# Two recurrences on one core: neighbouring chunks' state products issued in turn into two PSUM banks, and one pool of eight banks

## Chip, core and metric

The kernel runs on one core of a Trainium2 chip. The metric is the device time of one execution in microseconds (us), taken as the median of several runs. The engines are called as in the profile: PE (matrix products), PEld (the weight loads that go with them), DVE, ACT, POOL, and SP, whose queue issues most DMAs. PSUM, where products land, has eight banks here, each of 512 float32 values in 128 partitions.

## What is computed

Two blocks of two layers each act on 512 tokens of width 1024, all in float32. Almost all of the work is dense projections, cross-attention, sliding-window attention and feed-forward layers. One layer of each block holds a gated recurrence, computed by chunks. The first (HGRN2) has 4 heads, chunks of 32 tokens, key and value width 128:

```python
k_end = k * jnp.exp(b_last - b)
d_state = jnp.einsum('bhnsd,bhnsv->bhndv', k_end, v)   # state products, one per chunk and head
def step(state, inp):                                   # scan over the chunks
    dec, ds = inp
    return dec[..., None] * state + ds, state
...
o_inter = jnp.einsum('bhntd,bhndv->bhntv', q_t, s_start)
o = o_intra + o_inter
```

The second (GLA) has the same form with 4 heads, chunks of 64 tokens, key width 128 and value width 256.

## The kernel before

Tokens lie in four tiles of 128 (`t` = 0 to 3). Large projections are done at a split precision: each operand is a high and a low part in a 32-bit format that PE reads in one pass, and a product is three matmuls (`mm3`, lines 180 to 182). Weights arrive by DMA on SP, ACT makes the high part (line 152, or 172 with a gain) and DVE the low part (line 153 or 173). `lin_a` and `lin_b` hold four banks for one projection, with the contraction as the outer loop, and hand each bank to an evacuation on ACT or DVE at the end. `lin_out` with `between` (the output projections of the attentions and of the first mixer) holds four banks half accumulated while other work runs between its halves.

PSUM is divided by two pools. `bank` (line 125) takes projections, attention outputs and the readout's accumulator `po` from the pool `mm` of five banks; `xbank` (line 132) takes transposes, scores, cumulative sums and state products from the pool `aux` of three.

The program's text does not fix the order on the engines. A scheduler walks the instructions by priority (the text's order, moved by `high_priority`, `ahead` and `later`) against its own model of time, gives a tile a free bank of its pool when the first instruction on it is placed, and writes out one fixed order for each engine. On the chip each engine goes through its order and waits on semaphores.

The recurrence (`recur`, line 547) runs over the four tiles: `advance(t)` and then, one tile behind, `readout(t-1)`. `advance` transposes q and k (line 254, copied by ACT in lines 564 and 567), makes the scores of the four heads (line 570), masks them (line 573), and then goes over the chunks of the tile, four in HGRN2 and two in GLA. For each chunk the state products (line 581) of all its heads go into one bank (HGRN2) or two (GLA, two heads in each). A chunk's operands lie in its own rows: rows 0 to 31, 32 to 63 and so on in HGRN2, 0 to 63 and 64 to 127 in GLA, so that PE uses 32 or 64 rows of its array. Then DVE makes the new state of each head (line 588; line 586 for the first): old state times decay plus the product out of PSUM. `readout` adds the scores' part (line 605) and the states' part (line 608, one chunk's rows of the output at a time) in the bank `po`, and ACT squares and scales it (lines 612 and 616). The products are plain float32, and each stands in the trace as two records: 64 products in HGRN2 and 32 in GLA leave 192.

Beside the HGRN2 recurrence run the projections of its q and its gate, keys and values of the cross-attention, and a convolution of 31 taps, which DVE does in 90 instructions of low priority (line 525).

Of the kernel before, what the change touches and what calls it, by code (L numbers as in the profile page):

```python
# [10 lines left out]
F32 = mybir.dt.float32  # L11
# [3 lines left out]
ALU = mybir.AluOpType  # L15
# [57 lines left out]
class Net:  # L73
    def __init__(self, tc, a, ctx):
        self.tc, self.nc, self.a = tc, tc.nc, a
        pool = lambda name, bufs, **kw: ctx.enter_context(tc.tile_pool(name=name, bufs=bufs, **kw))
        self.const = pool("const", 1)
        self.wp = pool("wp", 4)
        self.rawp = pool("rawp", 3)
        self.big = pool("big", 16)  # L80
        self.work = pool("work", 2)
        self.small = pool("small", 4)
        self.mm = pool("mm", 5, space=bass.MemoryType.PSUM)
        self.aux = pool("aux", 3, space=bass.MemoryType.PSUM)
        self.n = 0
        nc = self.nc
        self.consts = self.const.tile([128, NCONST], F32, name="consts")
        nc.sync.dma_start(self.consts[:, :DEC], a["consts"][:, :DEC])
        self.ident = self.consts[:, IDENT:IDENT + 128]
        self.steps = self.const.tile([128, 256], F32R, name="steps")  # L90
        nc.scalar.activation(self.steps, self.consts[:, TRI:TRI + 256], AF.Copy)
        self.gains_T = self.const.tile([128, 40], F32, name="gains_T")
        self.half = self.const.tile([128, 8], F32, name="half")
        nc.gpsimd.memset(self.half, -0.5)
        self.r = []
        for t in range(4):
            self.r.append(self.const.tile([128, 1024], F32, name=f"r{t}"))
            nc.sync.dma_start(self.r[t], a["x"][0, t * 128:(t + 1) * 128, :])
            if t == 1:
                self.first = self.chunk(a["ab_w_in"][0], 2560, ahead=0)  # L100
# [29 lines left out]
        return bank  # L130

    def xbank(self, shape):
        return self.aux.tile(shape, F32, tag="aux", name=self.nm("aux"))

    def bload(self, dst, ap):
        self.nc.sync.dma_start(dst, ap.unsqueeze(0).broadcast_to(list(dst.shape)))
# [156 lines left out]
        else:  # L293
            self.nc.vector.tensor_tensor(r, r, ps, ALU.add)  # L294

# [1 line left out]

    def hgrn_mixer(self):
        nc, a = self.nc, self.a
# [259 lines left out]
    def advance(self, t, qt, kt, ke, vh, dec, before, tri, size, dv):  # L559
        nc = self.nc  # L560
        nch = 128 // size
        ps = self.transpose4(qt[:, t, :])
        qT = self.tmp().rearrange("p (h t) -> p h t", h=4)
        nc.scalar.activation(qT, ps, AF.Copy)
        ps = self.transpose4(kt[:, t, :])
        kT = self.tmp().rearrange("p (h t) -> p h t", h=4)
        nc.scalar.activation(kT, ps, AF.Copy)
        sc = self.xbank([128, 4, 128])
        for h in range(4):
            nc.tensor.matmul(sc[:, h, :], kT[:, h, :], qT[:, h, :], start=True, stop=True)  # L570
        P = self.masked[t % 2]
        mask = self.consts[:, tri:tri + 128].bitcast(I32).unsqueeze(1).broadcast_to([128, 4, 128])
        nc.vector.copy_predicated(P, mask, sc)
        new = self.slot([128, nch, 4, dv], name="S")
        per = 512 // dv
        for c in range(nch):
            rows = slice(c * size, c * size + size)
            for h0 in range(0, 4, per):
                d = self.xbank([128, per, dv])
                for h in range(h0, h0 + per):  # L580
                    nc.tensor.matmul(d[:, h - h0, :], ke[rows, t, h * 128:h * 128 + 128], vh(t, h)[rows, :],  # L581
                                     start=True, stop=True)
                for h in range(h0, h0 + per):
                    p = new[:, c - 1, h, :] if c else None if before is None else before[0][:, nch - 1, h, :]
                    if p is None:
                        nc.vector.tensor_copy(new[:, c, h, :], d[:, h - h0, :])
                    else:
                        nc.vector.scalar_tensor_tensor(new[:, c, h, :], p, dec[:, t, h, c:c + 1], d[:, h - h0, :],
                                                       ALU.mult, ALU.add)
        return new, qT, P  # L590

    def readout(self, t, got, before, vh, size, dv, out, po):
# [211 lines left out]
            first = False  # L804


# [1 line left out]

    def gla_prepare(self):
        nc, a = self.nc, self.a  # L810
# [312 lines left out]
```

## Time and profile before

| | before |
|---|---|
| runs | 2504.08, 2504.81, 2505.48 us (median 2504.81) |
| span of the profiled execution | 2503.4 us |
| PE busy | 2458.3 us (98%) |
| DVE busy | 1249.7 us (50%) |
| ACT busy | 944.6 us (38%) |
| POOL busy | 181.3 us (7%) |
| state products (line 581), PE busy | 30.4 us in 192 records |

The profiled execution has no time of its own beside its span. The span goes from its first to its last instruction, and the three runs lie 0.7 to 2.1 us above it. A busy PE is not PE at its peak, since matmuls overlap in the records: what an instruction costs is read from how far the next one starts behind it. PEclk is the share of its full clock that PE was granted.

### The profile page before, as it was taken

How to read it: one execution, taken by the hardware profiler on the slowest of the kernel's cores; microseconds unless marked ns; L12 is line 12 of the kernel's file. 1: busy time of each engine (PE TensorE's matmuls, PEld its weight loads, DVE VectorE, ACT ScalarE, POOL GpSimd, SP SyncE). 2: the span in 40 equal slices, each digit the busy share in tenths (PEclk: the TensorE clock that was granted, in tenths of full speed). 3: DMA queues.
4: the chain of work that ended last, by engine and by line, in shares of the span. 5: the costliest groups of instructions: out<-in, count | busy, mean ns of one | idle time of the engine just before them, and what ended most of it. 6: DMA issues, size and time to landing. Idle time of an engine off the chain costs nothing.

```text
span 2503.4 us, 30298 instructions
## 1 busy us (share of the span) xinstructions
PE 2458.3 (98%) x12334; PEld 2052.4 (82%) x12334; DVE 1249.7 (50%) x1772; ACT 944.6 (38%) x1576; POOL 181.3 (7%) x219
## 2 busy tenths in 40 slices
PE   8989999999999999999999999999999999999998
PEld 8876787888888997888888786888888877888887
DVE  4798566433326766433327423444444467444443
ACT  3643343222223343322224634433223456423323
POOL 1151300000000100000001003100000100000000
PEclk9999899999999999999999999999999999999999
DMA  6323122333324332233223223233222421222222
GB/s 214 109 102 102 53 85 77 92 99 95 99 74 144 123 130 76 85 101 99 95 76 121 69 85 43 76 101 101 93 101 98 142 74 51 72 97 95 99 93 84
DMA packets 121788, 239.48 MB, mean 96 GB/s; under 512 B 7849, under 2 KB 14309, under 8 KB 121392
## 3 DMA queue, kind: packets, MB, share of 16 engines
q1 hardware_dynamic: 118976, 229.73, 28.3%
q0 software_dynamic: 2096, 6.76, 1.4%
q8 instruction: 97, 1.59, 0.3%
q10 hardware_dynamic: 576, 1.05, 0.1%
q14 instruction: 43, 0.35, 0.0%
HBM read 234.34 MB, written 6.32 MB: 96 GB/s over the span
## 4 chain that ended last, share of the span: by engine, by line
PE 90%; DVE 6%; issue 1%; ACT 1%; DMA 1%; POOL 0%; SPq 0%; POOLq 0%; DVEq 0%; ACTq 0%
PE mm L180 28%; PE mm L181 27%; PE mm L182 27%; DVE acc L525 2%; PE aux L254 2%; PE aux L581 1%; DVE w L153 1%; PE aux L180 1%; PE mm L608 1%; PE mm L605 1%; PE aux L182 1%; PE aux L181 1%; DVE bn L275 0%; PE aux L1043 0%; DMA raw<-in_ffn_wg 0%
## 5 line engine op out<-in xcount | busy, mean ns | idle before, releaser
L153 DVE TENSOR_TENSOR w<-raw,w 128x1024 fp32r<-128x1024 f32 (+1 forms) x286 | 341.0, 1195 | 604.4 <-ACT w L152 604.1
L181 PE MATMUL mm<-xTl,w 128*128 128x512 f32 (+1 forms) x1696 | 614.0, 363 | 2.2 <-DVE xTl L153 2.2
L180 PE MATMUL mm<-xTh,w 128*128 128x512 f32 (+1 forms) x1696 | 610.4, 363 | 1.0 <-ACT w L152 0.8
L182 PE MATMUL mm<-xTh,w 128*128 128x512 f32 (+1 forms) x1696 | 605.7, 362 | 0.0
L152 ACT ACTIVATE w<-raw 128x1024 fp32r<-128x1024 f32 (+1 forms) x286 | 293.8, 1029 | 748.8 <-PE mm L182 598.3
L181 PEld LDWEIGHTS mm<-xTl,w 128*128 128x128 f32 x1696 | 321.5, 190 | 50.8 <-DVE xTl L153 2.4
L180 PEld LDWEIGHTS mm<-xTh,w 128*128 128x128 f32 x1696 | 320.9, 190 | 50.4 <-ACT w L152 1.2
L182 PEld LDWEIGHTS mm<-xTh,w 128*128 128x128 f32 x1696 | 319.4, 189 | 48.8
L181 PE MATMUL mm<-w,hidh 128*128 128x512 f32 x752 | 292.0, 389 | 0.0
L180 PE MATMUL mm<-w,hidh 128*128 128x512 f32 x752 | 291.1, 389 | 0.0
L182 PE MATMUL mm<-w,hidl 128*128 128x512 f32 x752 | 288.9, 389 | 0.0
L173 DVE SCALAR_TENSOR_TENSOR w<-raw,gains_T,w 128x512 fp32r<-128x512 f32 (+1 forms) x200 | 139.0, 738 | 212.0 <-ACT w L172 211.3
L172 ACT ACTIVATE w<-raw,gains_T 128x512 fp32r<-128x512 f32 (+1 forms) x200 | 131.3, 707 | 237.3 <-PE mm L182 220.9
L182 PEld LDWEIGHTS mm<-w,hidl 128*128 128x128 f32 x752 | 141.2, 188 | 29.3
L180 PEld LDWEIGHTS mm<-w,hidh 128*128 128x128 f32 x752 | 141.2, 188 | 29.2
L181 PEld LDWEIGHTS mm<-w,hidh 128*128 128x128 f32 x752 | 141.2, 188 | 29.1
L180 PE MATMUL mm<-w,xTh 128*128 128x512 f32 (+1 forms) x352 | 135.1, 386 | 0.0
L181 PE MATMUL mm<-w,xTh 128*128 128x512 f32 (+1 forms) x352 | 135.1, 384 | 0.0
L182 PE MATMUL mm<-w,xTl 128*128 128x512 f32 (+1 forms) x352 | 134.8, 384 | 0.0
L294 DVE TENSOR_TENSOR r<-r,mm 128x512 f32<-128x512 f32 x112 | 76.3, 686 | 72.8 <-PE mm L182 72.7
L525 DVE SCALAR_TENSOR_TENSOR acc<-u,pack,acc 128x511 f32<-128x511 f32 (+29 forms) x90 | 83.7, 972 | 0.0
L180 PEld LDWEIGHTS mm<-w,xTh 128*128 128x128 f32 x352 | 66.5, 189 | 15.5 <-issue 2.3
(323 smaller groups left out, 3344.9 us busy)
## 6 DMA issues: line engine op xcount, KB each, us to landing
raw<-in_w_up SPq DMA_DIRECT2D x64, 512.0 KB, 3.6
raw<-in_w_down SPq DMA_DIRECT2D x64, 512.0 KB, 3.2
raw<-in_ffn_wd SPq DMA_DIRECT2D x44, 512.0 KB, 3.2
raw<-in_ffn_wg SPq DMA_DIRECT2D x40, 512.0 KB, 3.6
raw<-in_ffn_wu SPq DMA_DIRECT2D x40, 512.0 KB, 3.5
raw<-in_ab_w_in SPq DMA_DIRECT2D x24, 512.0 KB, 3.8
raw<-in_a_w_in SPq DMA_DIRECT2D x24, 512.0 KB, 3.6
raw<-in_xa_wk SPq DMA_DIRECT2D x16, 512.0 KB, 3.3
```

The lines of the kernel that those rows point to most:

```text
L152: self.nc.scalar.activation(hi, src, AF.Copy)
L153: self.nc.vector.tensor_tensor(lo, src, hi.bitcast(F32), ALU.subtract)
L172: nc.scalar.activation(u[:, 0, i], raw[:, i], AF.Identity, scale=g)
L173: nc.vector.scalar_tensor_tensor(u[:, 1, i], raw[:, i], g, u[:, 0, i].bitcast(F32), ALU.mult, ALU.subtract)
L180: nc.tensor.matmul(ps, lh, rh, start=start, stop=False)
L181: nc.tensor.matmul(ps, lh, rl, start=False, stop=False)
L182: nc.tensor.matmul(ps, ll, rh, start=False, stop=stop)
L254: self.nc.tensor.transpose(ps[:, j, :], src[:, j * 128:j * 128 + 128], self.ident)
L294: self.nc.vector.tensor_tensor(r, r, ps, ALU.add)
L525: nc.vector.scalar_tensor_tensor(dst, src, col, dst, ALU.mult, ALU.add)
L581: nc.tensor.matmul(d[:, h - h0, :], ke[rows, t, h * 128:h * 128 + 128], vh(t, h)[rows, :], start=True, stop=True)
L605: nc.tensor.matmul(o, P[:, h, :], vh(t, h), start=True, stop=False)
```

## The change

```diff
-        self.mm = pool("mm", 5, space=bass.MemoryType.PSUM)
-        self.aux = pool("aux", 3, space=bass.MemoryType.PSUM)
+        self.mm = pool("mm", 8, space=bass.MemoryType.PSUM)
...
     def xbank(self, shape):
-        return self.aux.tile(shape, F32, tag="aux", name=self.nm("aux"))
+        return self.mm.tile(shape, F32, tag="mm", name=self.nm("aux"))
...
-        for c in range(nch):
-            rows = slice(c * size, c * size + size)
+        for c0 in range(0, nch, 2):
             for h0 in range(0, 4, per):
-                d = self.xbank([128, per, dv])
+                ds = [self.xbank([128, per, dv]) for _ in range(2)]
                 for h in range(h0, h0 + per):
-                    nc.tensor.matmul(d[:, h - h0, :], ke[rows, t, h * 128:h * 128 + 128], vh(t, h)[rows, :],
-                                     start=True, stop=True)
-                for h in range(h0, h0 + per):
-                    p = new[:, c - 1, h, :] if c else None if before is None else before[0][:, nch - 1, h, :]
-                    if p is None:
-                        nc.vector.tensor_copy(new[:, c, h, :], d[:, h - h0, :])
-                    else:
-                        nc.vector.scalar_tensor_tensor(new[:, c, h, :], p, dec[:, t, h, c:c + 1], d[:, h - h0, :],
-                                                       ALU.mult, ALU.add)
+                    for c, d in zip((c0, c0 + 1), ds):
+                        rows = slice(c * size, c * size + size)
+                        nc.tensor.matmul(d[:, h - h0, :], ke[rows, t, h * 128:h * 128 + 128], vh(t, h)[rows, :],
+                                         start=True, stop=True)
+                for c, d in zip((c0, c0 + 1), ds):
+                    for h in range(h0, h0 + per):
+                        p = new[:, c - 1, h, :] if c else None if before is None else before[0][:, nch - 1, h, :]
+                        if p is None:
+                            nc.vector.tensor_copy(new[:, c, h, :], d[:, h - h0, :])
+                        else:
+                            nc.vector.scalar_tensor_tensor(new[:, c, h, :], p, dec[:, t, h, c:c + 1],
+                                                           d[:, h - h0, :], ALU.mult, ALU.add)
```

The number of products, of DVE steps, of banks filled and of bytes moved stays the same. Two chunks that follow each other take a bank each, and their products are issued in turn, head by head. All PSUM tiles, those of `bank` and of `xbank`, come from one pool of eight.

## Rows read from the trace of the kernel before

**Rows 1.** The page: PE's busy time and the other engines'.

```profile
PE 2458.3 (98%) x12334; PEld 2052.4 (82%) x12334; DVE 1249.7 (50%) x1772; ACT 944.6 (38%) x1576; POOL 181.3 (7%) x219
```

**Rows 2.** Waits of PE: waiter and releaser; us in total, times, longest us.

```profile
PE mm L180 <- ACT oh L152: 4.2, 6, 1.5
PE mm L181 <- DVE w L153: 4.1, 5, 1.6
PE aux L535 <- DVE pack L545: 3.4, 1, 3.4
PE mm L180 <- DVE qt L368: 3.1, 1, 3.1
```

**Rows 3.** Windows: length, busy us (instructions) by engine, PEclk, DMA share, GB/s.

```profile
core 0: us, PE busy (x) PEld busy (x) DVE busy (x) ACT busy (x) POOL busy (x), PEclk, DMA share, GB/s
125.00:135.00 10.00, 6.58 (x26) 5.01 (x25) 10.00 (x11) 3.10 (x4) 6.12 (x4) 0.86 0.19 66
135.00:150.00 15.00, 11.81 (x71) 10.81 (x71) 15.00 (x22) 5.20 (x8) 5.45 (x3) 0.87 0.10 35
...
200.00:232.00 32.00, 31.97 (x187) 24.01 (x186) 32.00 (x61) 10.19 (x21) 3.47 (x2) 1.00 0.37 123
232.00:245.00 13.00, 12.89 (x110) 9.91 (x111) 9.21 (x26) 4.75 (x15) 1.21 (x2) 0.99 0.24 82
245.00:270.00 25.00, 23.46 (x151) 16.12 (x146) 7.58 (x25) 10.81 (x34) 12.92 (x13) 0.66 0.02 7
1484.00:1538.00 54.00, 53.02 (x261) 35.57 (x260) 21.70 (x44) 21.38 (x53) 10.36 (x17) 1.00 0.19 39
```

**Rows 4.** Chain that ended last, HGRN2: start us, us, what (line 581).

```profile
200.13 1.08 PE aux L581 x8
...
230.56 1.64 PE aux L581 x16
```

**Rows 5.** The same chain, GLA.

```profile
1484.17 1.92 PE aux L581 x8
...
1509.29 1.06 PE aux L581 x4
1510.78 1.06 PE aux L581 x4
1519.88 2.03 PE aux L581 x12
1524.34 1.06 PE aux L581 x4
```

**Rows 6.** Timeline of PE: start us, us, what [idle before, releaser]; lines 581 and 608.

```profile
237.18 0.41 PE L608 MATMUL mm<-S,tmp 128*32 128x128 f32 x2
...
237.94 0.42 PE L608 MATMUL mm<-S,tmp 128*32 128x128 f32 x8
...
240.93 3.52 PE L581 MATMUL aux<-v,ke 32*128 32x128 f32 x32
```

**Rows 7.** Line 581: what its engine's idle time before it ended with.

```profile
  DVE S L588: 1.0, 3
```

**Rows 8.** Timeline of DVE: the state steps of line 588.

```profile
209.82 1.11 DVE L588 SCALAR_TENSOR_TENSOR S<-S,pack,aux 128x128 f32<-128x128 f32 x4
...
212.77 1.11 DVE L588 SCALAR_TENSOR_TENSOR S<-S,pack,aux 128x128 f32<-128x128 f32 x4
...
242.12 4.22 DVE L588 SCALAR_TENSOR_TENSOR S<-S,pack,aux 128x128 f32<-128x128 f32 x16 [0.36 <-PE aux L581]
1490.83 1.74 DVE L588 SCALAR_TENSOR_TENSOR S<-S,consts,aux 128x256 f32<-128x256 f32 x4 [2.10 <-PE aux L581]
```

**Rows 9.** Timeline, end of the HGRN2 recurrence: last products, ACT, next readout.

```profile
252.25 4.03 PE L581 MATMUL aux<-v,ke 32*128 32x128 f32 x32
...
253.88 2.06 ACT L375 ACTIVATE g<-mm 128x512 f32<-128x512 f32 x4
...
257.02 0.80 PE L605 MATMUL mm<-v,pack 128*128 128x128 f32 x2 [0.74 <-ACT qt L616]
```

**Rows 10.** Timeline of PE: a readout of GLA that waits.

```profile
1527.40 0.70 PE L605 MATMUL mm<-v,pack 128*128 128x256 f32 x2 [0.98 <-ACT v L616]
```

## The prediction

> **What bounds the kernel now.** The page comes first: PE is busy for 2458.3 of 2503.4 us [rows 1], so only 45 us of the span have no matmul in flight, and a gain must come from fewer microseconds of PE's own work or out of those 45. Then PE's waits, which say what the idle time is made of. The reader is to see that three of the four large entries can be waits for PSUM: PE's cumulative sums wait 3.4 us for DVE's copy in line 545, which reads a bank of the pool of three; a projection waits 3.1 us for the DVE evacuation in line 368; and 4.2 us go in six waits to ACT's evacuation of attention outputs [rows 2]. Third, windows over the two recurrences, to see which engine sets the pace. From 125 to 232 us it is DVE, which in the windows shown is busy for their whole length (10.00 of 10.00, 15.00 of 15.00, 32.00 of 32.00). From 232 to 270 us DVE has gaps. In GLA PE is busy 53.02 of 54 us and DVE 21.70, so PE alone sets the pace [rows 3]. Last, the chain that ended last, for the price of the state products.
>
> **The products.** In HGRN2 one chunk alone, eight records, takes 1.08 us of the chain; two chunks one after the other, sixteen records, take 1.64 us and not 2.16 [rows 4]. So records of two row groups overlap already where the second chunk has a bank and follows directly: its eight records cost 0.56 us more. GLA says it more sharply. Eight records of one chunk take 1.92 us, four take 1.06, but twelve (eight of chunk 0 and four of chunk 1) take 2.03 [rows 5]: the four in the other row group cost 0.11 us in place of about 0.86 (1.92 − 1.06). The readout shows the same across columns, where eight records of four column groups end in 0.42 us, as two do in 0.41 [rows 6]. I take overlap at full rate as given; the question is how much of it has not been had yet, and who would notice.
>
> GLA: the chain holds three groups of 1.92, four of 1.06 and two of 2.03 [rows 5]: 5.76 + 4.24 + 4.06 = 14.06 us. After the change there are eight groups of two banks, each four records against four. One such group costs between 1.06 (the second chunk free) and 1.17 (plus 0.11); I take 1.10, 8.8 us in all, so −5.3 us. The worst case is that only the first pair of each tile finds two banks in time: 4 × (1.17 + 1.92) = 12.4, so −1.7. The best is that both groups of a tile run on without a break: 4 × (1.92 + 0.11) = 8.1, so −5.9. This lies on the path, since PE sets the pace there.
>
> HGRN2, tiles 0 and 1 (before 232 us): PE's saving falls into the stretch where DVE is full [rows 3]; PE would come earlier to waits on DVE. I put it at 0. Were DVE no cover, it would be 4 × 0.56 = 2.2 us at most for second chunks that now ride at 1.64, and a little more for the pieces issued singly. Tile 2: 32 records take 3.52 us [rows 6], two pairs would take 2 × 1.08, so −1.3. Tile 3: 4.03 us for the same, but the readout behind it starts at 257.02, when ACT has finished line 616, and ACT had been held by the gate's 2.06 us [rows 9]. A shorter product block changes nothing there: 0, with −1.9 (4.03 − 2.16) as its bound.
>
> The DVE steps are the same in number. What is late next is their chain: 16 steps of a tile take 4.22 us in a row [rows 8], longer than the products of a tile in either kernel. It stays covered by other PE work in GLA (DVE 21.70 of 54), and not at HGRN2's end.
>
> The Trainium skill weighs on this twice. "TensorE: Matmul & The Clock Gate", Part 3 on packing small matmuls, has matmuls of different row groups run side by side, a pack lasting as long as one matmul plus about 4 ns for each further tile. The rows agree in kind, with 0.11 us for four records of the other group; by the page's figure the GLA term would be an estimated −5.6 us in place of −5.3. Against the change speaks "TensorEngine Tiling (Array Packing)", PSUM Bottleneck: tiling speeds up TensorE, not the evacuation of PSUM, which may become the limit. At HGRN2's end the trace agrees (4.22 us of DVE against 3.52 of products); the second rival below is this case.
>
> **The shared pool.** In the attentions' output projections four banks are held while attention outputs are made, so the pool of five leaves them one, and each waits for the evacuation of the last. The 4.2 us of rows 2 are that wait. With eight banks up to three more are there; the evacuations' own latency stays, so I take half, −2 (bounds 0 and −4.2). The waits of 3.4 and 3.1 us would go with more banks, but both lie where DVE is full; PE would go on and meet DVE a little later. I take −1.5, with 0 as one bound and −6.5 as the other. PEclk is 0.86 and 0.87 in these two windows [rows 3]; over 25 us that is about 3.4 us of lost full-speed time (10 × 0.14 + 15 × 0.13), which widens the bound to −9.9. Elsewhere projections take four banks at a time and find them evacuated: PE's list of waits has no other large entry of this kind. The scheduler's order can shift anywhere in the kernel; I put its mean at 0 and its size at ±5, a ninth of all PE idle time.
>
> The end of HGRN2 runs at PEclk 0.66 over 25 us [rows 3], which is half clock for most of it, 8.5 us of lost full-speed time. The change alters both the density and the length of this stretch; nothing in the trace says which way, so 0, with 8.5 as the bound of a gain.
>
> **The sum.** −5.3 − 1.3 − 2 − 1.5 = −10.1 us. Against the profiled span that is 2493.3; the median of the runs lies 1.4 us above the span, so 2494.7 us.
>
> **Rivals.** First, more of it: PE does meet free banks and full clock. −5.3 − 1.3 − 4.2 − 9.9 and half of 8.5 give −25, or 2480 us. For it speaks that both long waits are followed by a stretch at half clock, against it that DVE is at 100% through them. Second, the saving is hidden: the evacuation on DVE and the readout's wait on ACT set the end. GLA's readout already waits 0.98 us on ACT [rows 10], and products done earlier then only lengthen such waits. GLA gives its worst case of 1.7, HGRN2 nothing, the pool 1: 2502 us, no change that can be measured. Against it: in GLA PE is busy 98% of the stretch.
>
> Third, slower: a pair holds a bank while it wants another. With a projection holding four banks and the readout's `po` one, three of eight are left, and the scores or a transpose take one of them. The first chunk's products of the next pair take the free bank, and the second's stand in PE's fixed order until DVE has read a bank of the pair before. Behind them on PE's queue are the projection's matmuls, and DVE in turn waits for those to evacuate. In HGRN2 two chunks' DVE steps start 2.95 us apart, with convolution in between [rows 8]; four pairs before 232 us would cost 11.8 us. In GLA a bank comes free after two steps, half of 1.74 [rows 8], so 0.87 for each tile's second group, 3.5 in all. Less the overlap that is left (1.7 + 1.3) that makes +12, or 2517 us. The products now wait only 1.0 us on line 588 [rows 7]; the case decides when that sum exceeds the some 10 us gained. Against it speaks that the same three banks sufficed before, and that nothing forces the scheduler to issue a pair's first half before its second can follow.
>
> **How the numbers follow.** The forecast (−5 to −20) has 0.50, the larger gain 0.17, the hidden one 0.20, the slower one 0.13. A difference under 0.2%, 5 us, can hardly be told from none in this kernel. Forecast and larger gain are faster: 0.67; the hidden one is the same: 0.20; slower: 0.13. The range reaches from 2484, which leaves out the far half of the larger gain, to 2507, which takes in the hidden case with the order's shift and leaves out the slower one. The forecast's own range is 2485 to 2500.
>
> **What would show it.** Right: eight records of GLA's two chunks in about 1.1 us of the chain and sixteen of HGRN2's in about 1.1 too; state products busy for under 22 us in place of 30.4; no wait of line 535 on line 545 and less than 2 us on ACT's attention outputs. Wrong: sixteen HGRN2 records that still take 1.64; a wait of line 581 on line 588 of more than 5 us; PE idle time that grows by what the products gave back; or a stretch at half clock that appears or goes, which moves the sum by up to 8.5 us in either direction.

## The result, and the profile after

The changed kernel takes 2881.71 us (median of four runs, 2876.16 to 2882.96); the kernel before, run beside it, 2504.9 us (median of four). The ratio is 1.1501, with an interval of 1.1484 to 1.1517. The prediction had 2494.7 us and a range up to 2507: it is wrong in sign, by 387 us from its forecast and by 375 us from the end of its range.

The page of the changed kernel: span, busy time by engine, and the clock granted to PE in 40 slices.

```profile
span 2878.8 us, 30269 instructions
...
PE 2582.1 (90%) x12334; PEld 2155.1 (75%) x12334; DVE 1268.4 (44%) x1772; ACT 952.1 (33%) x1576; POOL 189.1 (7%) x219
...
PEclk9997889899998788899998899889999888899999
```

PE issues the same 12334 instructions as before [rows 1]. Its idle time grows from 45.1 us (2503.4 − 2458.3) to 296.7 us (2878.8 − 2582.1), which is 251.6 us. Its busy time grows by 123.8 us (2582.1 − 2458.3), and the sum, 375.4 us, is the whole difference of the spans. The clock row tells where the second part is from: seventeen of 40 slices have a 7 or an 8. The mean clock granted over the span is 0.925, after 0.993.

What PE waited for in the changed kernel (waiter and releaser; us in total, times, longest). Lines before the recurrence have moved up by one, so L253 is L254 of before. The program still names the tiles of `xbank` aux, though their banks now come from the pool `mm`.

```profile
PE aux L253 <- ACT z L478: 77.5, 15, 9.0
PE aux L253 <- DVE r L286: 77.1, 16, 9.7
PE aux L253 <- DVE tmp L695: 22.1, 11, 3.6
PE aux L1044 <- DVE s L1030: 17.3, 5, 6.8
PE aux L443 <- DVE r L286: 15.5, 3, 5.2
PE aux L253 <- ACT qt L538: 11.8, 8, 6.6
...
PE aux L440 <- DVE r L286: 6.0, 1, 6.0
```

Before, the list's entries for waits on another engine were 4.2 us and less [rows 2]. Four of the lines above (z of L478, r of L286 into L253, L443 and L440) are one kind of place in the code: the end of an output projection or of the pooling layer's product, which I call the tail. There a tile of the result is finished, DVE, POOL and ACT normalize it, and PE transposes it (L253) or multiplies it by the bands of the pooling (L440, L443) for the next stage. 77.5 + 77.1 + 15.5 + 6.0 = 176.1 us in 35 waits; there are 36 such tiles.

None of them is a wait for a bank: the releasers are r and z, the normalized tile itself. PE stands in front of a transpose whose input isn't made yet. The timeline of PE in the changed kernel, in the tail of the first output projection (start, us, what [idle before, releaser]):

```profile
351.34 0.39 PE L181 MATMUL mm<-wb,yTl 128*128 128x512 f32 x1
356.94 1.89 PE L253 MATMUL aux<-consts,r 128*128 128x128 f32 x8 [5.21 <-DVE r L286]
358.48 0.78 PE L179 MATMUL mm<-wb,yTh 128*128 128x512 f32 x1
359.06 0.63 PE L180 MATMUL mm<-wb,yTh 128*128 128x512 f32 x1
359.48 0.63 PE L181 MATMUL mm<-wb,yTl 128*128 128x512 f32 x1
...
360.61 0.39 PE L181 MATMUL mm<-wb,yTl 128*128 128x512 f32 x1
360.84 0.40 PE L179 MATMUL mm<-wb,yTh 128*128 128x512 f32 x1
```

And DVE in that gap:

```profile
351.77 0.69 DVE L291 SCALAR_TENSOR_TENSOR r<-r,mm 128x512 f32<-128x512 f32 x1 [3.79 <-PE mm L181]
...
353.46 1.28 DVE L285 SCALAR_TENSOR_TENSOR r<-r,mv,w4k 128x1024 f32<-128x1024 f32 x1
355.51 1.28 DVE L286 SCALAR_TENSOR_TENSOR r<-r,rs,w4k 128x1024 f32<-128x1024 f32 x1 [0.76 <-POOL rs L268]
```

The last matmul of a tile ends at 351.73. Residual, statistics and normalization take from 351.77 to 356.79, and only then do the transposes start. The matmuls of the next tile, which need none of this, stand behind them. Then they begin at half clock: the starts of matmuls of 128x512 lie 0.42 us apart at 359 us and 0.23 from 360.6 on, which are the levels of 1.2 and 2.4 GHz (the granted clock is 0.52 from 356.90 to 360.30 us, and 1.00 from 360.70 to 365), and the tile's eight transposes take 1.89 us, in place of 1.04 in the kernel before.

The kernel before, same view, at the same place:

```profile
317.93 0.39 PE L182 MATMUL mm<-wb,yTl 128*128 128x512 f32 x1
318.16 1.04 PE L254 MATMUL aux<-consts,r 128*128 128x128 f32 x8
...
328.78 1.04 PE L254 MATMUL aux<-consts,r 128*128 128x128 f32 x8
```

There a tile's transposes come after other matmuls, at 328.78 us in the middle of the next stage's projection, and wait for nothing. The stretch of the loss and one without tails, in windows of the changed kernel (columns as in [rows 3]):

```profile
340.00:400.00 60.00, 41.09 (x226) 36.10 (x225) 25.61 (x34) 9.65 (x15) 8.32 (x8) 0.86 0.10 36
560.00:880.00 320.00, 320.00 (x1453) 266.65 (x1452) 113.94 (x126) 90.67 (x110) 0.66 (x1) 1.00 0.32 102
```

The products themselves did what was forecast. Line 581 in the changed kernel by shape (busy us, mean ns of one, idle before), and the first and last of its four GLA groups in the chain that ended last:

```profile
L581 PE MATMUL aux<-v,ke 32*128 32x128 f32 x128 | 14.2, 385 | 0.0
...
L581 PE MATMUL aux<-v,ke 64*128 64x256 f32 x64 | 8.0, 389 | 0.0
```

```profile
1744.45 1.93 PE aux L581 x16
...
1772.73 1.93 PE aux L581 x16
```

A tile's sixteen records of GLA products, both chunks, take 1.93 us, as long as eight of one chunk took before (1.92) [rows 5].

### The profile page after: what moved, and what is told of

Its sections match the earlier page's. It is cut to its first block, busy times and chain, and to the rows that moved or that the text cites. A ratio compares the mean times of both kernels' runs of the same rounds, so it can differ in the third digit from the quotient of the medians.

```text
span 2878.8 us, 30269 instructions
## 1 busy us (share of the span) xinstructions
PE 2582.1 (90%) x12334; PEld 2155.1 (75%) x12334; DVE 1268.4 (44%) x1772; ACT 952.1 (33%) x1576; POOL 189.1 (7%) x219
## 4 chain that ended last, share of the span: by engine, by line
PE 71%; ACT 4%; DVE 3%; POOL 2%; issue 1%; DMA 0%; POOLq 0%; ACTq 0%; DVEq 0%
PE mm L179 22%; PE mm L180 22%; PE mm L181 22%; PE aux L253 2%; DVE r L286 1%; POOL rs L265 1%; ACT z L478 1%; POOL rs L268 1%; ACT z L453 1%; DVE bn L274 1%; PE aux L1044 1%; PE aux L443 1%; DVE r L293 1%; ACT s L1022 1%; PE aux L179 1%
## 5 line engine op out<-in xcount | busy, mean ns | idle before, releaser
L179 PE MATMUL mm<-xTh,w 128*128 128x512 f32 (+1 forms) x1696 | 619.4, 365 | 0.0
L181 PE MATMUL mm<-xTh,w 128*128 128x512 f32 (+1 forms) x1696 | 616.8, 364 | 0.1
L181 PEld LDWEIGHTS mm<-xTh,w 128*128 128x128 f32 x1696 | 324.7, 191 | 49.6 <-DVE w L152 0.3
L179 PEld LDWEIGHTS mm<-xTh,w 128*128 128x128 f32 x1696 | 325.2, 192 | 48.8
L253 PE MATMUL aux<-consts,r 128*128 128x128 f32 x160 | 35.6, 398 | 83.2 <-DVE r L286 77.1
L151 ACT ACTIVATE xTh<-aux 128x512 fp32r<-128x512 f32 x72 | 42.3, 597 | 175.5 <-PE aux L253 175.5
```

The costliest lines, as they stand in the source:

```text
L151: self.nc.scalar.activation(hi, src, AF.Copy)
L179: nc.tensor.matmul(ps, lh, rh, start=start, stop=False)
L181: nc.tensor.matmul(ps, ll, rh, start=False, stop=stop)
L253: self.nc.tensor.transpose(ps[:, j, :], src[:, j * 128:j * 128 + 128], self.ident)
```

## The experiments

**Theory.** All banks come from one pool, and in one pool a tile that is written later in the text of the kernel gets its bank only after those written earlier have got theirs. So PE's order becomes the order of the text: matmuls of a tile, its transposes, matmuls of the next tile. With the transposes in a pool of their own the scheduler could put matmuls in front of them. **Rival one:** the pairs do it, by holding two banks. **Rival two:** the order in which banks are requested does it, and earlier requests would mend it.

**The two halves of the change.** The pairs alone, in the pools of five and three:

```diff
-                d = self.xbank([128, per, dv])
+                ds = [self.xbank([128, per, dv]) for _ in range(2)]
```

> Products in pairs as in the changed kernel, but the two pools of five and three banks kept. Theory (the shared pool alone made the loss, by putting PE's order into the order of the text): the loss is gone and the products' own gain is left, 2498 us (2492 to 2503), the product groups of GLA at about 1.1 us for eight records. Rival (the pairs hold banks and stall PE): at least 100 us of the 377 us stay, over 2600 us.

The pool alone, with the products chunk by chunk:

```diff
-        self.mm = pool("mm", 5, ...)
-        self.aux = pool("aux", 3, ...)
+        self.mm = pool("mm", 8, ...)
...
-        return self.aux.tile(shape, F32, tag="aux", name=self.nm("aux"))
+        return self.mm.tile(shape, F32, tag="mm", name=self.nm("aux"))
```

> The kernel before with one pool of eight banks and nothing else changed. Theory: the whole loss, 2887 us (2870 to 2905), a little over the changed kernel since the products' gain is missing. Rival (the pairs make the loss): under 2520 us.

Pairs alone: 2511.41 us, ratio 1.0025 (1.0012 to 1.0038). Pool alone: 2894.83 us, ratio 1.155 (1.1528 to 1.1572), with the tails' waits of the changed kernel:

```profile
PE aux L253 <- ACT z L478: 77.6, 15, 9.1
PE aux L253 <- DVE r L286: 77.1, 16, 9.7
```

The pool costs 390 us by itself, and rival one falls. Beside it pairs gain 13 us (2894.83 − 2881.71): chunk by chunk the products are busy for 19.3 + 16.6 = 35.9 us there, against 14.2 + 8.0 = 22.2 in the changed kernel (line 580 with the pool alone, 581 in the changed kernel).

```profile
L580 PE MATMUL aux<-v,ke 32*128 32x128 f32 x128 | 19.3, 398 | 0.0
L580 PE MATMUL aux<-v,ke 64*128 64x256 f32 x64 | 16.6, 509 | 0.0
```

That pairs lose 6 us in the old pools was a miss; it comes back below.

**Only the order of the text.** In the changed kernel the transposes of a finished tile are written later, behind the second half of the tile two further on; pool and pairs stay. Where the next stage takes a tile scaled by ACT (the z of L478), that scaling stands in `nxt` too and is written later with the transposes.

```diff
-        ev = self.tail(512, first, norm, nxt)
+        held = []
+        ev = self.tail(512, first, norm, held.append)
...
                 self.mm_b([p], [t], xT, ub, range(nk), nk)
+                if len(held) > 1:
+                    nxt(held.pop(0))
...
+        for t in held:
+            nxt(t)
```

> The changed kernel, one pool of eight, but in the output projections the transposes of a finished tile stand two steps later in the text, behind the matmuls of the next tiles. Theory (a pool grants its banks in the order of the text, so transposes that wait for their data hold back the matmuls that follow them): three of the four waits of each of eight output projections go, 110 us of waiting and about 40 us of half clock, 2730 us (2690 to 2780). Rival (eight banks in one pool run out, whatever the text's order): within 30 us of 2882.

2699.74 us, ratio 1.0772 (1.0752 to 1.0793): 182 us come back. The tails' waits, now on L258:

```profile
PE aux L258 <- DVE r L291: 39.0, 7, 9.6
...
PE aux L258 <- ACT z L483: 17.8, 6, 4.5
```

Thirteen of these waits are left, with 56.8 us. The timeline of PE, at the end of the first output projection:

```profile
359.03 1.91 PE L258 MATMUL aux<-consts,r 128*128 128x128 f32 x16
...
365.55 1.97 PE L258 MATMUL aux<-consts,r 128*128 128x128 f32 x8 [4.61 <-DVE r L291]
```

The first three tiles are transposed without a wait, two of them in the row at 359.03; the last one still waits, since no later tile's matmuls stand between. Four of the thirteen waits, 25.2 us, are the tails of the pooling layer, which calls `tail` by itself, so that this edit does not reach them.

**Only the requests.** In the changed kernel the banks of the next two steps are requested ahead of a tile's transposes; the matmuls stand where they stood.

```diff
+        steps = ((0, 0), (0, 1), (1, 0), (1, 1), (0, 2), (0, 3), (1, 2), (1, 3))
+        banks = []
+        for i, (half, t) in enumerate(steps):
+            while len(banks) < min(len(steps), i + 1 + 2):
+                h2, t2 = steps[len(banks)]
+                banks.append((ps[t2] if h2 == 0 else None) or self.bank([128, 512]))
```

> The changed kernel, but the output projections ask for the banks of the next two steps ahead of a tile's transposes; the matmuls stand in the text where they stood. Theory (a bank is granted in the order in which the first writers stand in the text): no change, 2882 us (2865 to 2900). Rival (the order of the requests decides): under 2750 us.

2883.82 us, ratio 1.1516 (1.1495 to 1.1537), and the same waits. Rival two falls: where a bank is asked for does not count. With the run before it, what counts is where the instructions that first write it stand in the text.

**Only the tails, in the kernel before.** Products, pairs and pools as before; the transposes and bands of the tails alone take their banks from the matmuls' pool of five.

```diff
-    def transpose4(self, src):
-        ps = self.xbank([128, 4, 128])
+    def transpose4(self, src, tail=False):
+        ps = self.bank([128, 4, 128]) if tail else self.xbank([128, 4, 128])
...
-                ps = self.xbank([128, 4, 128])
+                ps = self.bank([128, 4, 128])
```

> The kernel before, pools of five and three, products as before; only the transposes and bands that end the output projections take their banks from the pool of the projections. Theory: these alone bring their part of the loss, the 176 us of waits seen behind them in the changed kernel and their share of half clock, 2740 us (2690 to 2790). Rival (it needs the scores, products and cumulative sums in the same pool, or a shortage of banks): under 2530 us.

2777.18 us, ratio 1.1087 (1.1063 to 1.1112):

```profile
PE 2537.9 (91%) x12334; PEld 2114.4 (76%) x12334; DVE 1260.2 (45%) x1772; ACT 951.2 (34%) x1578; POOL 192.3 (7%) x219
```

```profile
PE mm L254 <- DVE r L287: 86.4, 16, 9.7
PE mm L254 <- ACT z L479: 77.0, 15, 8.8
PE mm L444 <- DVE r L287: 15.4, 3, 5.2
PE mm L441 <- DVE r L287: 6.1, 1, 6.1
```

These are the same 35 waits, 184.9 us, on the old kernel, and with five banks they are as many as with eight. Its span is 2774.7 us: 271.3 more than before, of which 191.7 are idle PE (236.8 − 45.1) and 79.6 busy PE. Divided by the waits, that is on average 2.3 us of slower matmuls behind each.

**Only the tails, taken out again.** In the changed kernel the eight banks become six shared and two for the tails.

```diff
-        self.mm = pool("mm", 8, ...)
+        self.mm = pool("mm", 6, ...)
+        self.tl = pool("tl", 2, ...)
```

> The changed kernel with its eight banks split six and two: the two are for the transposes and bands that end the output projections, everything else shares the six. Theory (banks are granted in the order of the text within a pool): the tails' part of the loss, about 270 us as measured with those transposes alone in the projections' pool, goes, and what is left is the same rule elsewhere (attention, cumulative sums, recurrences without projections beside them): 2620 us (2570 to 2660). Rival (eight shared banks are too few): with six for the rest it gets worse, over 2850 us.

2629.81 us, ratio 1.0495 (1.0476 to 1.0514), 252 us less than the changed kernel. The timeline of PE in the tail of the first output projection, and the largest waits that are left:

```profile
339.04 0.39 PE L180 MATMUL mm<-wb,yTh 128*128 128x512 f32 x1
339.27 1.04 PE L257 MATMUL tl<-consts,r 128*128 128x128 f32 x8
340.06 0.47 PE L181 MATMUL mm<-wb,yTh 128*128 128x512 f32 x1
```

```profile
PE aux L257 <- DVE tmp L699: 21.3, 10, 3.6
PE aux L1048 <- DVE s L1034: 10.6, 3, 5.7
...
PE aux L257 <- ACT qt L542: 8.3, 8, 3.2
```

The transposes stand between two matmuls of a tile and wait for nothing. The kernel has eight banks as before, and only six for all other uses, and is faster: it is not the number of banks that counts, but which uses share them. Some 124 us over the kernel before are left, of which 85.1 are idle PE (2627.5 − 2497.3 − 45.1):

```profile
PE 2497.3 (95%) x12334; PEld 2084.5 (79%) x12334; DVE 1260.5 (48%) x1772; ACT 952.5 (36%) x1578; POOL 184.0 (7%) x219
```

The largest waits are again transposes that wait for what they transpose (L257), or attention work that waits for DVE (L1048), in the six banks that other uses still share.

**Where the pairs lose in the old pools.** Pairs in the second recurrence only (`wide = 2 if dv == 256 else 1`), pools of five and three:

> Pools of five and three as before, pairs in the second recurrence alone, chunk by chunk in the first. Theory (the loss of 6 us with pairs in both comes from the first recurrence, whose end stays at half clock for longer): 2503 us (2498 to 2506). Rival (it comes from the second recurrence or from the shifted order behind it): 2508 us or more.

Pairs in the first only (`wide = 2 if dv == 128 else 1`):

> Pools of five and three, pairs in the first recurrence alone. Theory (the 6 us lost with pairs in both come from the first recurrence): 2509 us (2506 to 2514), with more time at half clock between 232 and 280 us than the kernel before. Rival (they come from the two together, or from the order elsewhere): 2505 us or less.

Second only: 2502.6 us, ratio 0.9987 (0.9976 to 0.9997). First only: 2512.52 us, ratio 1.0031 (1.0018 to 1.0043). The products of the second recurrence, busy us in the kernel with pairs there alone:

```profile
L584 PE MATMUL aux<-v,ke 64*128 64x256 f32 x64 | 12.2, 401 | 0.0
```

and in its chain that ended last:

```profile
1482.80 1.06 PE aux L584 x8
...
1487.49 1.06 PE aux L584 x4
```

The products took 14.7 us in the kernel before, and 8.0 with eight shared banks. With three banks the first pair of this tile goes through in 1.06 us and of the second only one chunk at a time, four records in 1.06, which is the pattern of the prediction's worst case (12.4 us): 2.5 us are gained over all tiles, and the run is 3.05 us shorter than the kernel before beside it (2505.65). It is the fastest kernel here, by an amount that measurement hardly tells from none.

In the first recurrence the end runs at half clock. Windows at that end, with pairs there alone, then the kernel before:

```profile
232.00:285.00 53.00, 50.47 (x299) 36.48 (x298) 20.42 (x55) 17.75 (x52) 15.00 (x17) 0.71 0.07 23
...
245.00:275.00 30.00, 28.68 (x151) 19.56 (x152) 8.61 (x28) 11.05 (x34) 11.70 (x12) 0.50 0.02 5
```

```profile
232.00:285.00 53.00, 50.89 (x327) 37.66 (x327) 25.33 (x62) 20.84 (x56) 16.60 (x19) 0.84 0.10 31
```

0.13 of clock over 53 us is an estimated 6.9 us, nearly the 8 us lost. PE is about as busy as before (50.47 and 50.89 us); why the chip holds 1.2 GHz there for 30 us is not settled.

**Four and four.** If three banks are too few for pairs, two pools of four might do. The attention outputs and the sliding window's `po` move to the second pool, and the gate projections take tiles in two halves.

```diff
-        self.mm = pool("mm", 5, ...)
-        self.aux = pool("aux", 3, ...)
+        self.mm = pool("mm", 4, ...)
+        self.aux = pool("aux", 4, ...)
...
-                    ps = self.bank([128, 512])
+                    ps = self.xbank([128, 512])
...
-        po = self.ready(self.bank([128, 4, 128]))
+        po = self.ready(self.xbank([128, 4, 128]))
```

With pairs:

> Pairs of products in pools of four and four: the attention outputs and the sliding window's accumulator come from the second pool, and the gates' projections hold two banks at a time in place of four, so that nothing that must run side by side needs more than four of either. Theory (pairs gain when two banks are free for them, and three banks were one too few): 2499 us (2491 to 2506), GLA's products at most 10 us in all against 14.06. Rival (the pairs' gain goes into half clock and waits at the end of the first recurrence, whatever the banks): 2507 us or more.

With the same pools, chunk by chunk:

> The same pools of four and four with the products chunk by chunk as in the kernel before, to price the split by itself. Theory: 2504 us (2497 to 2511), so that the pairs are worth 3 to 8 us beside it. Rival (a projection misses its fifth bank): over 2515 us.

2529.29 us, ratio 1.009 (1.0072 to 1.0109), and 2533.34 us, ratio 1.0114 (1.0098 to 1.013). Both miss, and both rivals' signs came (2507 us or more, over 2515 us). The split alone costs 28 us, of which the list of waits of the kernel with pairs shows some:

```profile
PE mm L181 <- DVE w L173: 12.6, 1, 12.6
...
PE mm L180 <- DVE qt L368: 7.1, 1, 7.1
```

Pairs gain 4 us beside it, in place of a loss of 6 in five and three; the two ratios' intervals overlap, so the 4 us are hardly clear of noise. Since the split costs more than the pairs can give back, these two runs don't tell why pairs lose with three banks.

## Why the prediction was wrong, point by point

**The step that failed** is in the part on the shared pool: "The scheduler's order can shift anywhere in the kernel; I put its mean at 0 and its size at ±5, a ninth of all PE idle time." It measured +390 us (the pool alone). The shift isn't random: it comes at 35 of the 36 tiles of the tails, and always toward the text's order. The bound was taken from the idle time of a kernel whose order was good, which says how little there is to gain and nothing of what a worse order costs. A view that pointed at it was there: in the trace of before, transposes that the text has ahead of the next projection are issued in its middle, without a wait; something let them change places with its matmuls, and the change puts exactly these two uses into one pool. The price could have been estimated as well: 36 tiles, each with a chain of DVE, POOL and ACT between its last matmul and its transposes, which cost about 5 us a tile in waits (176.1 in 35).

**GLA products, −5.3.** Line 581 fell from 14.7 to 8.0 us there, −6.7; by the chain four groups of 1.93 make 7.7 in place of 14.06, −6.4, a little beyond the bound of −5.9. Eight records of the other row group, issued in turn, add 0.01 us (1.93 against 1.92). The 0.11 us that I took as the price of overlap came from four records that followed a chunk; issued in turn with it, they have no such price. By the Trainium skill ("TensorE: Matmul & The Clock Gate", Part 3) eight further tiles would add an estimated 0.03 us; the rows lie below even that, and here they decide. (By the same figure the prediction's sum makes 14.06 − 8 × 1.076 = 5.5, where it has 5.6.) But the saving came with eight shared banks, at 390 us; with three it is 2.5.

**HGRN2 products, −1.3.** Line 581 takes 14.2 us there in place of 15.7, though at half clock for part of the time (mean 385 ns of a record, in place of 291 before). At full clock (granted 1.00 from 208.60 to 210.40 us) the first tile's 32 records took less than the 2.16 us (2 × 1.08) that the prediction gave to two pairs:

```profile
208.69 1.72 PE L581 MATMUL aux<-v,ke 32*128 32x128 f32 x32
```

The sum itself is off a little: 3.52 − 2.16 is 1.36. In pools of five and three the pairs cost 8 us there; in the sum the clock was left at 0 with a bound of a gain only, and a loss of that size took place.

**Attention outputs and long waits, −2 and −1.5.** The waits on attention outputs and on line 368, and that of line 535 on line 545, are gone from the list of the changed kernel, as forecast; the cumulative sums wait 4.9 us for a split in line 152 instead (L535, line 536 of before). It doesn't show in the time, which has 251.6 us of new idle PE.

**The rivals.** The slower one was right in sign and wrong in place. It asked for more than 5 us of waits of line 581 on DVE's state steps; the changed kernel has, by what its engine's idle time before line 581 ended with,

```profile
  DVE S L589: 0.4, 1
```

one wait of 0.4 us. It priced banks held by a pair, +12 us; the loss is an order of transposes far from the recurrences. Of the signs set for "right", the waits came, eight records of GLA's two chunks take 1.06 us where they go as a pair, and with pairs in the old pools sixteen records of HGRN2 take 1.09 us in place of 1.64; the products' busy time just missed its sign (22.2 us, where it asked for under 22). Of the four signs set for "wrong", the last two came: idle time that grows by more than the products gave back, and stretches at half clock. Their bound of 8.5 us was far too small, as 123.8 us of busy time show.

**Shown and argued.** Shown: the shared pool is the cause, the tails moved alone cost 272 us of the pool's 390, taken out alone they give back 252 of the whole change's 377, the order of the text sets PE's order there, the order of requests doesn't. Argued: how the scheduler comes to this order inside, which no run shows; that the other 124 us are the same rule in other places, since their waits look alike, but no run took them apart; and that the 8 us of the first recurrence's pairs are the clock.

## What to carry to other kernels

Pools of PSUM are not only storage: with this scheduler two uses that shared one pool came out in the order of the text, and in separate pools it could reorder them. Before merging pools, list for each use what its first instruction waits for; a use that waits for other engines (a transpose behind a normalization) should not share with independent matmuls, or should be written later. The idle time of the old order says how much a better order can gain, and nothing of what a worse one costs.

## What the runs showed of the hardware

In these runs a gap cost more than its length. Behind 5.21 us of idle PE the changed kernel's matmuls started 0.42 us apart in place of 0.23, and over the kernel with the tails moved 191.7 us of gaps brought 79.6 us of slower matmuls. Small products in the other row group, issued in turn with the first, cost hardly anything that the trace can show (1.93 us for sixteen records, 1.92 for eight).
